# Fixed program order for TensorE from the third gMLP gate block to the last value block, with two S5 read-outs placed by hand

## Chip, core and metric

The kernel runs on one core of one Trainium2 chip. The metric is the device time of one execution in microseconds; "before" is the median of three runs, and one execution more was profiled.

## The reference

One decoder layer on 1024 tokens of width 1024, in fp32, as three sub-layers. Each is `x = x + rmsnorm(f(rmsnorm(x)))`. What matters here is the first one and the start of the second:

```python
h = rmsnorm(x, g_mix_pre)
s_in, s_gate, g_u, g_vv = split(h @ w_in)              # 4 x 512 columns
y_ssm  = gelu(s5_ssm(s_in, ...)) * sigmoid(s_gate)     # diagonal state space, 32 groups
y_gmlp = g_u * (tril(w_s) @ norm(g_vv) + b_s)          # per chunk of 128 positions
x = x + rmsnorm(concat(y_ssm, y_gmlp) @ w_out, g_mix_post)
mem_n = rmsnorm(mem, g_mem)                            # 256 memory tokens
k, v = mem_n @ w_k, mem_n @ w_v                        # for the cross-attention that follows
```

A gated ConvFFN ends the layer.

## The kernel before

**Layout.** Activations lie transposed, features on the partitions, tokens in two halves `h` of 512. Every fp32 matrix product is made of three fp32r products (hi x hi, hi x lo, lo x hi): `mm3` issues them, 24 for a block of eight 128-row parts. A weight tile comes by DMA into one of 4 `raw` slots; ScalarE casts it to its hi part (L132) and VectorE subtracts to get the lo part (L135), both into `w`, which has 13 slots. All DMAs are issued by SyncE (SP) from one queue, in order.

**S5.** The state space is computed in 8 batches of 4 groups by the generator `s5_batch`, in six steps: tables (VectorE and GpSimd), products and transposes into `px`, `pk`, the drive `pv`, rotation and scan (L588 to L600), turning back (L606 to L608), and the read-out: 8 products into an `sx` bank (L618, L619), which need L608. ScalarE then applies GELU (L621) and the result goes to memory as `yd`. `s5_all` starts a batch every second step, so the last read-outs, of batches 6 and 7, are traced in steps 17 and 19. For each block of 128 channels `s5_final` loads `yd` of two batches back in another layout (8 DMAs) with the sigmoid gate `gd`, multiplies (L659, half on VectorE, half on GpSimd), and splits the product into parts 0 to 3 of `mix`. Block 3 needs batches 6 and 7.

**The stage in question.** `mixers` runs in this order: columns for S5 and its gate, `gv`, gate blocks 0 and 1, mixing, gate blocks 2 and 3 (`gates(b)`, a product for each half, acc<-b), then 8 key blocks (acc<-m, 256 tokens wide) and 8 value blocks (acc<-w,m: 4 columns `c`, 2 memory halves `mt`). The memory is normalized in four pairs in `mem_parts` on VectorE (L686), ScalarE and GpSimd (L254, m<-sq,m), while the gates run. S5's steps, `mem_parts` and other side jobs advance by `tick`, called from `mm3`.

**Behind it.** `attention` begins with the output projection `o1`: 8 blocks for each half, which read the mix parts in the order 4, 5, 6, 7, 0, 1, 2, 3. Beside the first half GpSimd splits keys and values (`kv_parts`, kv<-m) and adds up tiles of the down-projection's weights for the last stage (`s_sums`: loads L1376, sums L1380, stores L1381). `sumsq` squares every block on ScalarE and adds the squares on GpSimd (L713, ac<-ac,sq); the total of the first half goes through TensorE (L281) while the second half's products run.

**What sets the order.** The kernel is traced, and a scheduler then orders every engine's queue by its own estimate of when operands are ready. An instruction given to `keep_in_program_order` is tied behind the one traced before it on its engine. `pin` does so, only while `self.pinned` is set, which is at the very end of the kernel. Engines run their queues in order.

Of the kernel before, what the change touches and what calls it, by code (L numbers as in the profile page):

```python
# [22 lines left out]
P = 128  # L23
# [17 lines left out]
WARM = 10  # L41
EARLY = 1
MIX_AT = 2
Q_STATS = (99, 3)
TAIL_R = (0, 7)
TAIL_B = (1, 3)
# [106 lines left out]
class Builder:  # L153
    def __init__(self, tc, a, out):
        self.tc = tc
        self.nc = tc.nc
        self.a = a
        self.out = out
        self.sides = []
        self.pools = []  # L160
        self.n_slot = 0
        self.pinned = False
        self.final_ok = False


    def slot(self, tag, dt=F32, shape=None):
# [56 lines left out]
    def pin(self, ins):  # L223

        if self.pinned:
            self.tc.keep_in_program_order(ins)

    def mm3(self, ps, parts, ticks=2, first=True, last=True, go_on=False):

        nc = self.nc  # L230
        n = len(parts)
        for i, (lh, ll, rh, rl) in enumerate(parts):
            for j, (x, y) in enumerate(((lh, rh), (lh, rl), (ll, rh))):
                self.pin(nc.tensor.matmul(ps, lhsT=x, rhs=y, start=first and i + j == 0,  # L234
                                          stop=last and i == n - 1 and j == 2, skip_group_check=go_on))
            if ticks and (i + 1) * ticks // n > i * ticks // n:
                self.tick()
# [297 lines left out]
    def s5_batch(self, b):  # L535

        nc, v, g = self.nc, self.nc.vector, self.nc.gpsimd
        g0 = 4 * b
        bq = 4 * (b % 2)
        gs = slice(g0, g0 + 4)  # L540
        q4 = lambda: self.slot("x", shape=[P, 4, P])

        def outer(o, A, B):
            t = q4()
            o4 = o.rearrange("p g (j c) -> p g j c", c=16)
            t4 = t.rearrange("p g (j c) -> p g j c", c=16)
            def av(x):
                return x[:, gs].unsqueeze(2).to_broadcast([P, 4, 8, 16])
            def bv(x):
                return x[:, :, gs].rearrange("p j g -> p g j").unsqueeze(3).to_broadcast([P, 4, 8, 16])  # L550
            v.tensor_tensor(o4, av(A[0]), bv(B[0]), ALU.mult)
            g.tensor_tensor(t4, av(A[1]), bv(B[1]), ALU.mult)
            v.tensor_tensor(o, o, t, ALU.add)
        xt = q4()
        outer(xt, self.s5_B, self.s5_G)
        yield
        px = self.bank("sx")
        pk = self.bank("sx")
        for i in range(4):
            nc.tensor.transpose(px[:, i * P:(i + 1) * P], xt[:, i], self.ident)  # L560
        for i in range(4):
            nc.tensor.matmul(pk[:, 16 * i:16 * i + 16], lhsT=xt[:, i], rhs=self.s5_c0[:, g0 + i], start=True, stop=True)
        x = q4()
        nc.scalar.copy(x.rearrange("p a b -> p (a b)"), px)
        ka = self.tiny([P, 16, 4], "s5ka", 2)
        v.tensor_tensor(ka, pk[:, :64].rearrange("p (g c) -> p c g", c=16),
                        self.s5_dd[:, gs].rearrange("p g c -> p c g"), ALU.add)
        kd = self.kd[b % 4]
        nc.sync.dma_start(kd[0:P], ka.rearrange("p c g -> p (c g)"))
        u = q4()  # L570
        nc.sync.dma_start(u, self.ud[b // 2].rearrange("j (c g) k -> (j c) g k", g=8)[:, bq:bq + 4])
        yield
        pv = self.bank("sx")
        for i in range(4):
            nc.tensor.matmul(pv[:, i * P:(i + 1) * P], lhsT=x[:, i], rhs=u[:, i], start=True, stop=True)
        vv = q4()
        nc.scalar.copy(vv.rearrange("p a b -> p (a b)"), pv)
        vs = q4()
        nc.sync.dma_start(vs[0:64], vv[64:P])
        nc.sync.dma_start(vs[64:P], vv[0:64])  # L580
        yield

        c, s, t = q4(), q4(), q4()
        f4 = lambda x: x.rearrange("p g (h l) -> p g h l", l=8)
        hv = lambda x: x[:, :, gs].rearrange("p h g -> p g h").unsqueeze(3).to_broadcast([P, 4, 16, 8])
        lv = lambda x: x[:, :, gs].rearrange("p l g -> p g l").unsqueeze(2).to_broadcast([P, 4, 16, 8])
        (lc, ls), (hc, hs) = self.s5_el, self.s5_eh
        g.tensor_tensor(f4(c), hv(hc), lv(lc), ALU.mult)  # L588
        g.tensor_tensor(f4(t), hv(hs), lv(ls), ALU.mult)
        v.tensor_tensor(c, c, t, ALU.subtract)  # L590
        t = q4()
        g.tensor_tensor(f4(s), hv(hc), lv(ls), ALU.mult)
        v.tensor_tensor(f4(t), hv(hs), lv(lc), ALU.mult)
        v.tensor_tensor(s, s, t, ALU.add)
        v.tensor_tensor(vv, vv, c, ALU.mult)
        v.tensor_tensor(vs, vs, s, ALU.mult)
        v.tensor_tensor(vv, vv, vs, ALU.add)
        w = t
        for i in range(4):
            v.tensor_tensor_scan(w[:, i], self.s5_r8[:, g0 + i:g0 + i + 1].to_broadcast([P, P]), vv[:, i], 0.0,  # L600
                                 ALU.mult, ALU.add)
        ws = vs
        nc.sync.dma_start(ws[0:64], w[64:P])
        nc.sync.dma_start(ws[64:P], w[0:64])
        yield
        v.tensor_tensor(w, w, c, ALU.mult)  # L606
        g.tensor_tensor(ws, ws, s, ALU.mult)
        v.tensor_tensor(w, w, ws, ALU.subtract)  # L608
        tz = self.slot("x", shape=[P, 8, 64])
        k0 = kd[0:1]  # L610
        nc.sync.dma_start(tz, bass.AP(k0.tensor, k0.offset, [[64, P], [16 * 64, 8], [1, 64]]))
        z = q4()
        outer(z, self.s5_C, self.s5_H)
        yield
        py = self.bank("sx")
        for i in range(4):
            o = py[:, i * P:(i + 1) * P]
            nc.tensor.matmul(o, lhsT=tz.rearrange("p j (c g) -> p (j c) g", g=4)[:, :, i], rhs=u[:, i], start=True, stop=False)  # L618
            nc.tensor.matmul(o[:, 1:P], lhsT=z[:, i], rhs=w[:, i, 0:P - 1], start=False, stop=True)  # L619
        y = q4()  # L620
        nc.scalar.activation(y.rearrange("p a b -> p (a b)"), py, AF.Gelu_apprx_tanh)  # L621
        nc.sync.dma_start(self.yd[b // 2].rearrange("j c g k -> (j c) g k")[:, bq:bq + 4], y)
        yield

    def s5_all(self):

        live = []
        b = 0
        step = 0
        while b < 8 or live:  # L630
            if b < 8 and step % 2 == 0:
                live.append(self.s5_batch(b))
                b += 1
            for gname in list(live):
                if next(gname, "end") == "end":
                    live.remove(gname)
            step += 1
            yield

    def s5_chain(self):  # L640
        yield from self.s5_all()
        while not self.final_ok:
            yield
        yield from self.s5_final()

    def s5_final(self):

        nc, v = self.nc, self.nc.vector
        for blk in range(4):
            y = [self.slot("k", shape=[P, 4, P]) for _ in range(2)]  # L650
            for j in range(8):
                nc.sync.dma_start(y[j // 4][:, j % 4], self.yd[blk][7 - j].rearrange("c g k -> (c g) k"))
            for h in range(2):
                sg = self.slot("k")
                nc.sync.dma_start(sg, self.gd[blk][h])
                sv = sg.rearrange("p (k j) -> p j k", j=8)
                for jh in range(2):
                    e = v if jh == 0 else nc.gpsimd
                    e.tensor_tensor(sv[:, 4 * jh:4 * jh + 4], y[jh][:, :, 64 * h:64 * h + 64],  # L659
                                    sv[:, 4 * jh:4 * jh + 4], ALU.mult)  # L660
                hl = self.mix[blk, h] = self.pair("b")
                self.split(*hl, sg)
                yield
# [233 lines left out]
    def mixers(self):  # L897
        nc, a, w, ids, xg = self.nc, self.a, self.w, self.ids, self.xg
        v, g = nc.vector, nc.gpsimd
# [4 lines left out]
        for kt in range(KT):  # L904
            if kt % 2 == 0:
                whi, wlo = w.get(ids["s01"][kt // 2])
            for h in range(2):
                hi, lo = hl = self.pair("b")
                x = self.xs[kt, h]
# [4 lines left out]
            for h in range(2):  # L914
                rh, rl = xg[h][kt]
                for b in range(2):
                    if kt == 0:
                        pss[b, h] = self.bank()
                    o = pss[b, h]
                    c = slice(256 * (kt % 2) + P * b, 256 * (kt % 2) + P * b + P)  # L920
# [38 lines left out]
        for b in range(4):  # L959
            part = self.blocks(ids["sg"][b])  # L960
            for h in range(2):
                ps = self.bank()
# [67 lines left out]
                mixing(b, h)  # L1030
        vt.clear()
        mem = self.side(self.mem_parts(), 1)
        for b in range(MIX_AT, 4):
            gates(b)
        xg[0], xg[1] = [], []
# [9 lines left out]
        for b in range(8):  # L1045
# [4 lines left out]
                self.kraw.append(self.slot("m", shape=[P, 2, 256]))  # L1050
            nc.scalar.copy(self.kraw[-1][:, b % 2], ps)
        for c in range(4):
            part = self.blocks(ids["v"][c], 256)
            for mt in range(2):
                ps = self.bank()[:, :256]
# [3 lines left out]
                nc.scalar.copy(self.vraw[mt, c // 2][:, 256 * (c % 2):256 * (c % 2) + 256], ps)  # L1059
        self.memp = None  # L1060
        self.drain(s5)


    def attention(self):
# [591 lines left out]
```

## Time and profile before

| | us |
|---|---|
| median of 3 runs (lowest, highest) | 1342.07 (1339.8, 1346.27) |
| profiled execution | 1340.39 |
| its span, first to last instruction | 1338.7 |
| TensorE busy in the span | 1270.3 |
| VectorE busy | 1062.5 |
| GpSimd busy | 691.0 |
| ScalarE busy | 628.3 |

Mean granted TensorE clock: 0.977. In a row of the trace stand start, length, engine, line, operation, out<-in, shapes, count, and in brackets the idle time ahead of it with what ended it. PE is TensorE, DVE VectorE, ACT ScalarE, POOL GpSimd. Lines are those of the kernel before; lines of the changed kernel stand 6 to 15 higher.

### The profile page before, as it was taken

How to read it: one execution, taken by the hardware profiler on the slowest of the kernel's cores; microseconds unless marked ns; L12 is line 12 of the kernel's file. 1: busy time of each engine (PE TensorE's matmuls, PEld its weight loads, DVE VectorE, ACT ScalarE, POOL GpSimd, SP SyncE). 2: the span in 40 equal slices, each digit the busy share in tenths (PEclk: the TensorE clock that was granted, in tenths of full speed). 3: DMA queues.
4: the chain of work that ended last, by engine and by line, in shares of the span. 5: the costliest groups of instructions: out<-in, count | busy, mean ns of one | idle time of the engine just before them, and what ended most of it. 6: DMA issues, size and time to landing. Idle time of an engine off the chain costs nothing. (4 is left out here: it accounts for less than half of the span.)

```text
span 1338.7 us, 19253 instructions
## 1 busy us (share of the span) xinstructions
PE 1270.3 (95%) x6356; PEld 1076.9 (80%) x6356; DVE 1062.5 (79%) x1627; ACT 628.3 (47%) x1176; POOL 691.0 (52%) x523
## 2 busy tenths in 40 slices
PE   9989998779999999889999999999999999999995
PEld 7778987678888788678888878888888888788885
DVE  7968989987558766996657988889998878995477
ACT  7233421245455444454545645555555555546341
POOL 1685445747644734630443838755565315763135
PEclk9989999879999999899999999999999999999997
DMA  9474435348826973451358566645555359666234
GB/s 319 139 206 113 114 95 166 86 125 306 288 94 200 319 244 89 125 187 56 91 163 296 162 222 233 186 144 161 154 167 164 103 162 379 190 201 210 72 92 157
DMA packets 150661, 233.56 MB, mean 174 GB/s; under 512 B 33697, under 2 KB 43041, under 8 KB 150561
## 3 DMA queue, kind: packets, MB, share of 16 engines
q1 hardware_dynamic: 150560, 232.34, 54.5%
q8 instruction: 49, 0.80, 0.3%
q14 instruction: 52, 0.42, 0.1%
HBM read 174.23 MB, written 53.85 MB: 170 GB/s over the span
## 5 line engine op out<-in xcount | busy, mean ns | idle before, releaser
L234 PE MATMUL acc<-b,w 128*128 128x512 f32 x2484 | 597.5, 393 | 10.0 <-DVE sq L965 3.4
L234 PEld LDWEIGHTS acc<-b,w 128*128 128x128 f32 x2484 | 466.6, 190 | 109.1 <-DVE sq L965 3.8
L135 DVE TENSOR_TENSOR w<-raw,w 128x512 fp32r<-128x512 f32 x206 | 203.9, 1000 | 92.6 <-PE acc L234 43.1
L234 PE MATMUL sx<-b,w 128*128 128x512 f32 x873 | 210.1, 390 | 0.7 <-ACT T L1303 0.6
L132 ACT CAST w<-raw 128x512 fp32r<-128x512 f32 x228 | 140.9, 621 | 132.7 <-PE acc L234 70.7
L234 PEld LDWEIGHTS sx<-b,w 128*128 128x128 f32 x873 | 163.6, 188 | 35.5 <-ACT T L1303 1.0
L234 PE MATMUL acc<-T,w 128*128 128x512 f32 x528 | 127.0, 389 | 0.0
L713 POOL TENSOR_TENSOR ac<-ac,sq 128x512 f32<-128x512 f32 x45 | 69.1, 1537 | 103.9 <-ACT sq L712 58.0
L234 PEld LDWEIGHTS acc<-T,w 128*128 128x128 f32 x528 | 99.1, 188 | 20.6
L254 DVE TENSOR_TENSOR w<-b,w 128x512 fp32r<-128x512 f32 x64 | 65.2, 1027 | 30.1 <-PE st L234 15.5
L731 POOL TENSOR_TENSOR m<-m,t 128x512 f32<-128x512 f32 x24 | 40.0, 1698 | 63.7 <-DVE m L730 50.7
L234 PE MATMUL sx<-T,w 128*128 128x512 f32 x264 | 66.5, 389 | 0.0
L234 PEld LDWEIGHTS sx<-T,w 128*128 128x128 f32 x264 | 49.6, 188 | 10.3
L712 ACT ACTIVATE sq<-m 128x512 f32<-128x512 f32 x66 | 41.0, 630 | 34.7 <-DVE ac L713 14.4
L116 POOL TENSOR_TENSOR st<-st,b 128x512 f32<-128x512 f32 x20 | 26.8, 1339 | 56.0 <-DMA st<-in_w_up 35.6
L1242 POOL TENSOR_TENSOR b<-b,m 128x512 f32<-128x512 f32 x22 | 32.2, 1466 | 44.9 <-ACT m L1241 44.7
L253 ACT CAST w<-b 128x512 fp32r<-128x512 f32 x64 | 39.6, 620 | 29.5 <-PE acc L234 18.1
L135 POOL TENSOR_TENSOR w<-raw,w 128x512 fp32r<-128x512 f32 x22 | 30.2, 1377 | 42.5 <-ACT w L132 24.7
L234 PE MATMUL acc<-w,b 128*128 128x256 f32 x384 | 49.3, 285 | 0.0
L1380 POOL TENSOR_TENSOR m<-m,m 128x512 f32<-128x512 f32 x28 | 39.3, 1410 | 18.9 <-DMA m<-in_w_dk 8.4
L730 DVE SCALAR_TENSOR_TENSOR m<-m,gains,st 128x512 f32<-128x512 f32 x32 | 44.5, 1457 | 3.3 <-ACT st L311 3.2
L234 PEld LDWEIGHTS acc<-w,b 128*128 128x128 f32 x384 | 47.0, 191 | 0.1
(360 smaller groups left out, 2335.5 us busy)
## 6 DMA issues: line engine op xcount, KB each, us to landing
raw<-in_w_up SPq DMA_DIRECT2D x68, 256.0 KB, 2.9
cd<-fd SPq DMA_DIRECT2D x44, 256.0 KB, 2.9
b<-sd SPq DMA_DIRECT2D x44, 256.0 KB, 3.9
b<-in_w_up SPq DMA_DIRECT2D x40, 256.0 KB, 2.8
raw<-in_w_out SPq DMA_DIRECT2D x32, 256.0 KB, 2.9
raw<-in_w_q SPq DMA_DIRECT2D x32, 256.0 KB, 2.8
raw<-in_w_o SPq DMA_DIRECT2D x32, 256.0 KB, 2.8
m<-in_w_dk SPq DMA_DIRECT2D x28, 256.0 KB, 4.7
```

The costliest lines, as they stand in the source:

```text
L116: g.tensor_tensor(p["S4"], p["12"], p["S2"], ALU.subtract)
L132: nc.scalar.copy(hi[:, :w], t[:, :w])
L135: e.tensor_tensor(lo[:, :w], t[:, :w], hi[:, :w], ALU.subtract)
L234: self.pin(nc.tensor.matmul(ps, lhsT=x, rhs=y, start=first and i + j == 0, stop=last and i == n - 1 and j == 2, skip_group_check=go_on))
L253: self.nc.scalar.copy(hi, src)
L254: (e or self.nc.vector).tensor_tensor(lo, src, hi, ALU.subtract)
L712: nc.scalar.activation(sq, src, AF.Square)
L713: (e or nc.gpsimd).tensor_tensor(acc, acc, sq, ALU.add)
L730: v.scalar_tensor_tensor(x, x, self.gain[gpost][:, i:i + 1], bc, ALU.mult, ALU.mult)
L731: g.tensor_tensor(x, x, rs, ALU.add)
L1242: nc.gpsimd.tensor_tensor(val, val, gate, ALU.mult)
L1380: g.tensor_tensor(t[to], t[x], t[y], op)
```

## The change

While `self.fixed` is set, from gate block 2 to the end of `mixers`, the products of `mm3` and of the read-outs keep the program's order. `s5_all` now halts at step 17 until the mix parts 4 to 7 are split (`final_ok`, just ahead of the key blocks), and at step 19 it first runs `s5_final` for blocks 0 to 2 and then halts until value column 2 begins (`v_ok`). Block 3 of `s5_final` follows at the end.

```diff
+V_AT = 2
...
+    def fix(self, ins):
+
+        if self.pinned or self.fixed:
+            self.tc.keep_in_program_order(ins)
...
-                self.pin(nc.tensor.matmul(ps, lhsT=x, rhs=y, start=first and i + j == 0,
+                self.fix(nc.tensor.matmul(ps, lhsT=x, rhs=y, start=first and i + j == 0,
...
         while b < 8 or live:
+
+            while step == 17 and not self.final_ok:
+                yield
+            if step == 19:
+                yield from self.s5_final(range(3))
+                while not self.v_ok:
+                    yield
...
     def s5_chain(self):
         yield from self.s5_all()
-        while not self.final_ok:
-            yield
-        yield from self.s5_final()
+        yield from self.s5_final(range(3, 4))
...
+        self.fixed = True
         for b in range(MIX_AT, 4):
             gates(b)
...
         for c in range(4):
+            self.v_ok = c >= V_AT
```

The order of instructions changes in one stretch of every queue and is the old one before and after it.

TensorE, read-out of batch 6 (sx), before: it stands in the last gate product, behind its first three instructions (b are the gates' operands).

```order
L234 MATMUL acc<-b_330,w_2512 128x512
L234 MATMUL acc<-b_331,w_2512 128x512
L234 MATMUL acc<-b_330,w_2513 128x512
L619 MATMUL sx<-x_1780,x_1827 128x127
L618 MATMUL sx<-x_1718,x_1825 128x128
L619 MATMUL sx<-x_1780,x_1827 128x127
L618 MATMUL sx<-x_1718,x_1825 128x128
L619 MATMUL sx<-x_1780,x_1827 128x127
L618 MATMUL sx<-x_1718,x_1825 128x128
L619 MATMUL sx<-x_1780,x_1827 128x127
L234 MATMUL acc<-b_358,w_2512 128x512
```

TensorE, the same read-out after the change (m are the normalized memory's pairs, m_2784 the last of them).

```order
L240 MATMUL acc<-m_2784,w_2560 128x256
L240 MATMUL acc<-m_2785,w_2560 128x256
L240 MATMUL acc<-m_2784,w_2561 128x256
L624 MATMUL sx<-x_1718,x_1825 128x128
L626 MATMUL sx<-x_1780,x_1827 128x127
L624 MATMUL sx<-x_1718,x_1825 128x128
L626 MATMUL sx<-x_1780,x_1827 128x127
L624 MATMUL sx<-x_1718,x_1825 128x128
L626 MATMUL sx<-x_1780,x_1827 128x127
L624 MATMUL sx<-x_1718,x_1825 128x128
L626 MATMUL sx<-x_1780,x_1827 128x127
L240 MATMUL acc<-m_2714,w_2704 128x256
```

It now follows the whole of key block 0. All 72 gate products from the second half of gate block 2 on, and key block 0, run ahead of it.

TensorE, read-out of batch 7, before: in the middle of key block 5.

```order
L234 MATMUL acc<-m_2793,w_3177 128x256
L234 MATMUL acc<-m_2794,w_3177 128x256
L619 MATMUL sx<-x_1860,x_1901 128x127
L618 MATMUL sx<-x_1808,x_1899 128x128
L619 MATMUL sx<-x_1860,x_1901 128x127
L618 MATMUL sx<-x_1808,x_1899 128x128
L619 MATMUL sx<-x_1860,x_1901 128x127
L618 MATMUL sx<-x_1808,x_1899 128x128
L619 MATMUL sx<-x_1860,x_1901 128x127
L234 MATMUL acc<-m_2793,w_3178 128x256
```

After: among the value products (w is the first operand there), between the two memory halves of value column 2.

```order
L240 MATMUL acc<-w_3454,m_2784 128x256
L240 MATMUL acc<-w_3455,m_2784 128x256
L240 MATMUL acc<-w_3454,m_2785 128x256
L624 MATMUL sx<-x_1808,x_2989 128x128
L626 MATMUL sx<-x_2940,x_2991 128x127
L624 MATMUL sx<-x_1808,x_2989 128x128
L626 MATMUL sx<-x_2940,x_2991 128x127
L624 MATMUL sx<-x_1808,x_2989 128x128
L626 MATMUL sx<-x_2940,x_2991 128x127
L624 MATMUL sx<-x_1808,x_2989 128x128
L626 MATMUL sx<-x_2940,x_2991 128x127
L240 MATMUL acc<-w_3409,m_2714 128x256
```

It moves from ahead of 61 key products and all values to behind all keys and five of the eight value blocks; three value blocks are left behind it. On VectorE and GpSimd batch 7's rotation and scan move behind the splits of more key weights and of mix parts 4 to 7, and blocks 0 to 2 of `s5_final` come earlier.

GpSimd, the output projection's first half, before (t<-t are the sums of down-projection weights, ac<-ac,sq the sums of squares of blocks 1 to 7).

```order
L1380 TENSOR_TENSOR t_3919<-t_3919,t_3917 128x512
L1380 TENSOR_TENSOR t_4023<-t_4021,t_4023 128x512
L713 TENSOR_TENSOR ac_3691<-ac_3691,sq_3748 128x512
L1380 TENSOR_TENSOR t_4021<-t_4017,t_4021 128x512
L1380 TENSOR_TENSOR t_4017<-t_4023,t_4017 128x512
L1380 TENSOR_TENSOR t_4019<-t_4019,t_4017 128x512
L713 TENSOR_TENSOR ac_3691<-ac_3691,sq_3806 128x512
L713 TENSOR_TENSOR ac_3691<-ac_3691,sq_3864 128x512
L713 TENSOR_TENSOR ac_3691<-ac_3691,sq_3914 128x512
L713 TENSOR_TENSOR ac_3691<-ac_3691,sq_3964 128x512
L713 TENSOR_TENSOR ac_3691<-ac_3691,sq_4014 128x512
L713 TENSOR_TENSOR ac_3691<-ac_3691,sq_4064 128x512
```

After:

```order
L1395 TENSOR_TENSOR t_3809<-t_3815,t_3809 128x512
L1395 TENSOR_TENSOR t_3917<-t_3923,t_3917 128x512
L725 TENSOR_TENSOR ac_3691<-ac_3691,sq_3914 128x512
L1395 TENSOR_TENSOR t_3811<-t_3811,t_3809 128x512
L1395 TENSOR_TENSOR t_4023<-t_4021,t_4023 128x512
L1395 TENSOR_TENSOR t_3919<-t_3919,t_3917 128x512
L725 TENSOR_TENSOR ac_3691<-ac_3691,sq_3964 128x512
L1395 TENSOR_TENSOR t_4021<-t_4017,t_4021 128x512
L725 TENSOR_TENSOR ac_3691<-ac_3691,sq_4014 128x512
L1395 TENSOR_TENSOR t_4017<-t_4023,t_4017 128x512
L1395 TENSOR_TENSOR t_4019<-t_4019,t_4017 128x512
L725 TENSOR_TENSOR ac_3691<-ac_3691,sq_4064 128x512
```

All sums of squares but one stood behind the weight sums; now the two are mixed to the end, and the last square's sum, which L281 reads, follows all 16 weight sums. In SP's queue the loads of those weights move behind ten of the projection's first weight tiles.

More of the change, by code (lines that the diff above doesn't have):

```diff
@@ L162, in __init__ @@
         self.pinned = False
-        self.final_ok = False
+        self.final_ok = self.v_ok = self.fixed = False
     def slot(self, tag, dt=F32, shape=None):
@@ L617, in s5_batch @@
             o = py[:, i * P:(i + 1) * P]
-            nc.tensor.matmul(o, lhsT=tz.rearrange("p j (c g) -> p (j c) g", g=4)[:, :, i], rhs=u[:, i], start=True, stop=False)
-            nc.tensor.matmul(o[:, 1:P], lhsT=z[:, i], rhs=w[:, i, 0:P - 1], start=False, stop=True)
+            self.fix(nc.tensor.matmul(o, lhsT=tz.rearrange("p j (c g) -> p (j c) g", g=4)[:, :, i], rhs=u[:, i],
+                                      start=True, stop=False))
+            self.fix(nc.tensor.matmul(o[:, 1:P], lhsT=z[:, i], rhs=w[:, i, 0:P - 1], start=False, stop=True))
         y = q4()
@@ L641, in s5_chain, with s5_final @@
         yield from self.s5_all()
-        while not self.final_ok:
-            yield
-        yield from self.s5_final()
-    def s5_final(self):
+        yield from self.s5_final(range(3, 4))
+    def s5_final(self, blocks):
         nc, v = self.nc, self.nc.vector
-        for blk in range(4):
+        for blk in blocks:
             y = [self.slot("k", shape=[P, 4, P]) for _ in range(2)]
@@ L1061, in mixers @@
         self.drain(s5)
+        self.fixed = False
     def attention(self):
```

## Prediction

> **What bounds the kernel now.** I read the page's busy shares first, then the table of stretches, the list of who waited for whom on TensorE, and last TensorE, VectorE and GpSimd in order of time where the change begins.
>
> ```profile
> PE 1270.3 (95%) x6356; PEld 1076.9 (80%) x6356; DVE 1062.5 (79%) x1627; ACT 628.3 (47%) x1176; POOL 691.0 (52%) x523
> 227.00:328.00 101.00, 81.73 (x519) 76.00 (x518) 86.55 (x87) 38.30 (x75) 66.39 (x44) 0.88 0.53 165
> 233.00:255.00 22.00, 12.11 (x53) 9.77 (x54) 21.34 (x26) 4.32 (x8) 15.05 (x11) 0.87 0.40 106
> 264.00:291.00 27.00, 19.13 (x131) 18.23 (x130) 26.33 (x26) 12.19 (x25) 18.36 (x11) 0.86 0.32 97
> PE sx L619 <- DVE x L608: 17.1, 5, 9.9
> PE acc L234 <- DVE w L135: 7.2, 7, 2.6
> ```
>
> TensorE bounds the kernel as a whole, but not from 227 to 328 us, where the change lies: there it idles 19 us in 101 (81.73 busy). In the rows of stretches the length is followed by the busy times of TensorE, its weight loads, VectorE, ScalarE and GpSimd, then the granted clock and the DMA columns. VectorE has 21.34 of 22.00 us and 26.33 of 27.00 us: in this stage it is the full engine, and TensorE waits for it. Of the read-outs' waits (17.1 us in all) 13.7 are the last two.
>
> ```profile
> 232.98 11.82 PE L234 MATMUL acc<-b,w 128*128 128x512 f32 x51
> 254.69 0.80 PE L619 MATMUL sx<-x,x 128*128 128x127 f32 x2 [9.89 <-DVE x L608]
> 257.76 5.85 PE L234 MATMUL acc<-b,w 128*128 128x512 f32 x21
> 265.13 7.79 PE L234 MATMUL acc<-m,w 128*128 128x256 f32 x63
> 290.79 0.80 PE L619 MATMUL sx<-x,x 128*128 128x127 f32 x2 [3.83 <-DVE x L608]
> 293.86 8.97 PE L234 MATMUL acc<-m,w 128*128 128x256 f32 x61
> 302.66 13.84 PE L234 MATMUL acc<-w,m 128*128 128x256 f32 x114
> 327.98 0.63 PE L234 MATMUL acc<-b,w 128*128 128x512 f32 x2
> 330.02 50.88 PE L234 MATMUL acc<-b,w 128*128 128x512 f32 x223 [1.42 <-DVE w L135]
> 380.75 0.95 PE L281 MATMUL st<-ones,ac 128*128 128x1 f32 x8
> ```
>
> acc<-b is a gate (to 263 us) or the output projection (from 328 us), acc<-m a key block, acc<-w,m a value block, sx a read-out. One product costs 11.82/51 = 0.232 us in the gates, 50.88/223 = 0.228 in the projection, 13.84/114 = 0.121 in the values. L281 is the sum of squares of the projection's first half: the last place that the change can move against its neighbours, since the order of every engine is the old one from about there.
>
> **Read-out 6 goes behind key block 0.** The 9.89 us wait for it disappears. What is late next is key block 0 itself.
>
> ```profile
> 259.78 1.29 POOL L254 TENSOR_TENSOR m<-sq,m 128x512 fp32r<-128x512 f32 x1
> 254.56 2.89 DVE L686 SCALAR_TENSOR_TENSOR sq<-sq,gains,ac 128x256 f32<-128x256 f32 x2
> ```
>
> 72 gate products are left at 232.98, so the gates end at 232.98 + 72 x 0.232 = 249.7. Key block 0 needs all of the normalized memory, and its last quarter is written by GpSimd until 261.07, from what VectorE ends at 257.45. Nothing on VectorE, GpSimd or ScalarE ahead of these rows is moved, and VectorE is full there. In program order TensorE therefore stands in key block 0, in three pieces, for 261.07 + 5 x 0.124 - 249.7 - 24 x 0.124 = 9.0 us (0.124 = 7.79/63) and ends it at 261.7. The read-out behind it (257.76 - 254.69 = 3.07 us) ends at 264.8. Before, key block 1 began at 265.13 + 13 x 0.124 = 266.7. Gain here: 1.9 us of the 9.9.
>
> **The key blocks** are fed by VectorE, whose queue is now: more weights first, batch 7's rotation and scan later.
>
> ```profile
> 260.45 1.62 DVE L593 TENSOR_TENSOR x<-k,k 128x512 f32<-128x512 f32 x1
> 281.09 2.45 DVE L600 TENSOR_TENSOR_SCAN x<-r,x 128x128 f32<-128x128 f32 x4
> 286.56 0.69 DVE L606 TENSOR_TENSOR x<-x,x 128x512 f32<-128x512 f32 x1 [0.64 <-DMA x<-x]
> 294.27 0.68 DVE L135 TENSOR_TENSOR w<-raw,w 128x512 fp32r<-128x512 f32 x1
> ```
>
> From 260.45 to 294.9 VectorE worked without a pause but the 0.64. By the time it splits the last weight of value block 0 it has, in the new order, done the same instructions less L606 and L608 (1.3 us) and that pause, plus three more splits (1.8): 294.8. A weight load starts when the split four places back is done, and by that two of these splits come up to 0.9 late: 295.7. This is a reordering of a full engine; the weights' waits in the key blocks grow by what the read-outs' waits shrink. Value block 0's last six products follow: 296.4, against 302.66 + 24 x 0.121 = 305.6 before. The gain is 9.2 us at this point.
>
> **Value blocks and read-out 7.** VectorE is ahead from here. Read-out 7 at full clock took 2.5 us:
>
> ```profile
> 221.73 0.49 PE L619 MATMUL sx<-x,x 128*128 128x127 f32 x2
> 224.21 2.07 PE L1013 MATMUL acc<-k,m 128*64 128x128 f32 x26
> ```
>
> Products after a wait are slow for a time: 61 took 8.97 us where 0.121 each gives 7.4, so I put 1.5 us on the first blocks. Four blocks (24 x 0.121 = 2.9 each), 1.5 and 2.5 put the read-out's end at 312.0; three more blocks end the values at 320.8. From there 225 products x 0.228 lead to L281: 372.1, against 380.75. Were TensorE alone, the gain would be 8.6 us.
>
> **What hangs on read-out 7.** It ended at 293.86 and will end at 312.0, 18 us later. Its chain is y to memory, eight loads back, gate, split into the last parts of the mix, and then on GpSimd the splits of keys and values and the sums of the down-projection's weights.
>
> ```profile
> 310.29 0.68 DVE L254 TENSOR_TENSOR b<-k,b 128x512 fp32r<-128x512 f32 x1
> 312.03 7.64 POOL L254 TENSOR_TENSOR kv<-m,kv 128x512 fp32r<-128x512 f32 x5 [3.36 <-ACT kv L253]
> 329.38 4.68 POOL L1380 TENSOR_TENSOR t<-t,t 128x512 f32<-128x512 f32 x3
> 334.01 3.00 POOL L254 TENSOR_TENSOR kv<-m,kv 128x512 fp32r<-128x512 f32 x2
> 336.99 7.86 POOL L1380 TENSOR_TENSOR t<-t,t 128x512 f32<-128x512 f32 x5
> 344.80 1.74 POOL L713 TENSOR_TENSOR ac<-ac,sq 128x512 f32<-128x512 f32 x1
> 346.51 4.68 POOL L1380 TENSOR_TENSOR t<-t,t 128x512 f32<-128x512 f32 x3
> 351.15 1.28 POOL L713 TENSOR_TENSOR ac<-ac,sq 128x512 f32<-128x512 f32 x1
> 375.25 1.29 POOL L713 TENSOR_TENSOR ac<-ac,sq 128x512 f32<-128x512 f32 x1 [4.15 <-ACT sq L712]
> t<-in_w_dk SPq DMA_DIRECT2D x16, 256.0 KB, 5.4
> POOL m L1380 <- DMA m<-in_w_dk: 8.4, 2, 4.6
> L1380 POOL TENSOR_TENSOR m<-m,m x28: 1265/1295/1808, 432.4 to 484.5; 128x512 f32<-128x512 f32 x28
> ```
>
> The last mix part is ready 310.29 + 0.68 - 293.86 = 17.1 us after the read-out (about 16.6 for the first half of the tokens, which goes first). TensorE asks for it 72 x 0.121 + 35 x 0.228 = 16.7 us after: 0, at most 1 us.
>
> GpSimd is the term that decides. Its run of 8 key/value splits, 16 weight sums and 7 sums of squares (31 in a row, the last one needed by L281) began 312.03 - 293.86 = 18.2 us after the read-out; before, it was through by 352.43 but for sums that waited on TensorE, the last at 376.5, 4.2 us ahead of L281. Now it begins at 312.0 + 18.2 = 330.2, with the sums of squares among the rest. Beside the projection's weight splits, 15 of these instructions took 352.43 - 329.38 = 23.05 us, 1.54 each; 31 take 47.6 us: 377.8. TensorE stands at L281 from 372.1, 5.7 us. Bounds: 1.29 (375.25's row, alone) gives 370.2 and no wait; 1.74 (344.80's) gives 384.1. I take 1.54, the same work in the same stage. L281 then runs 380.75 - 377.8 = 3.0 us earlier than before.
>
> After a wait of 9.89 us the 21 products took 5.85 us instead of 21 x 0.228 = 4.8 and the read-out 3.07 instead of 2.5: 1.6 us. The new wait costs the same; bounds 0 and 2.1 (read-out 7 and the 61 products, after 3.83 us).
>
> Sum: -8.6 + 5.7 + 1.6 = -1.3 us, and from there the old order shifts as a whole. The profiled execution takes 1340.39 us (span 1338.7 and 1.7 around it), inside the runs' 1339.8 to 1346.27; it would take 1339.1. Against the median of 1342.07: 1340.8. About 0.5% (6.7 us) is what a measurement of this kernel can tell from no change.
>
> **Rivals.**
> *GpSimd keeps up* (faster). At 1.35 us each or less its 31 end by 372.1, and the whole 8.6 stays: 1333.5. For it: the later weight sums (the last row above, ns: least, median, most) have a median of 1.295 us. Against: 15 in 23.05 us here.
>
> *VectorE and GpSimd exclude each other* (no change, on the slow side). Each projection block brings two weight splits on VectorE, about 0.60 each when they follow each other, per 5.5 us. If none overlapped with GpSimd, 31 x 1.29 + 17 x 0.60 = 50.2 us, L281 at 380.4 and with the slow products +1.3: 1343.4. In 329.38 to 352.43 that sum gives 15 x 1.29 + 9 x 0.6 = 24.8, measured 23.05: most of it, not all. This is what the Trainium skill says in "SBUF — State Buffer", section "Who interferes with whom": a VectorE instruction with two SBUF inputs and a GpSimd one that reads SBUF share an exclusive lock. By that rule the time is the 1343.4 above; the trace shows slightly less.
>
> *GpSimd starves* (slower). The 16 weight-sum loads now stand in SP's queue behind the projection's weights, the last ones behind stores that wait for GpSimd. Each lands 5.4 us after its issue. If three of the four groups of loads hold GpSimd for 3.5 us, L281 comes 10.5 us later: 1351. It decides slower from 8 us of such waits. For it: GpSimd waited 8.4 us for two such loads later in the old kernel (the row of L1380 above). Against: each group of loads stands in the queue among the stores of the groups before it, so it is asked for while GpSimd still works on those.
>
> **How the numbers follow.** My forecast 0.53 (1340.8; own range 1336 to 1345), exclusion 0.15 (1343.4), GpSimd keeps up 0.21 (1333.5), starving 0.11 (1351). Faster by over 0.5%: the third and its like, 0.21; slower: the last, 0.11; within: 0.68. Range 1333 to 1347, which leaves out most of the starving case and half of the fast one's tail.
>
> **What would show it.** The profile after should have no wait of sx on L608 over 1 us from 233 us on; waits inside key block 0 for GpSimd and ScalarE, together near 9 us; L281 waiting some 6 us on GpSimd's L713; the values' end near 321 us, L281 near 378. I am wrong if L281 does not wait (the gain stays), if GpSimd has pauses for loads of w_dk, or if the key blocks' weights come before 290 us.

## The result, and the profile after

The changed kernel takes 1335.96 us (median of 17 runs, 1333.73 to 1341.39), the kernel before in the same session 1344.87 (17 runs, 1338.65 to 1352.68): ratio 0.9939, 95% interval 0.9922 to 0.9955, which is 8.2 us less (6.1 to 10.5). The forecast was 1340.8.

TensorE in order of time, after the change (start, length, count; in brackets the wait and what ended it). Lines have moved: L240 is the product, L287 the sum of squares (L281 before), L314 the next small product (L308 before).

```profile
249.06 1.59 PE L240 MATMUL acc<-m,w 128*128 128x256 f32 x12
...
254.19 1.44 PE L240 MATMUL acc<-m,w 128*128 128x256 f32 x5 [2.93 <-POOL m L260]
258.21 0.58 PE L240 MATMUL acc<-m,w 128*128 128x256 f32 x1 [2.58 <-ACT m L259]
261.14 1.43 PE L240 MATMUL acc<-m,w 128*128 128x256 f32 x5 [2.34 <-POOL m L260]
...
265.72 11.05 PE L240 MATMUL acc<-m,w 128*128 128x256 f32 x86
278.13 1.70 PE L240 MATMUL acc<-m,w 128*128 128x256 f32 x12 [1.37 <-DVE w L136]
281.52 3.13 PE L240 MATMUL acc<-m,w 128*128 128x256 f32 x24 [1.69 <-DVE w L136]
...
291.71 15.18 PE L240 MATMUL acc<-w,m 128*128 128x256 f32 x120
...
309.38 8.87 PE L240 MATMUL acc<-w,m 128*128 128x256 f32 x72
318.09 51.19 PE L240 MATMUL acc<-b,w 128*128 128x512 f32 x225
372.15 1.44 PE L287 MATMUL st<-ones,ac 128*128 128x1 f32 x8 [2.87 <-POOL ac L725]
373.46 10.58 PE L240 MATMUL acc<-b,w 128*128 128x512 f32 x33
383.87 1.05 PE L314 MATMUL st<-ident,rs_y 128*128 128x128 f32 x8
```

The 9.89 us wait for read-out 6 is gone. In its place key block 0 stands for 2.93, 2.58 and 2.34 us and, in a row left out, 0.23: 8.1 us. The key blocks then run with 4.3 us of waits for weights; the two longest are shown. The value blocks begin at 291.71, the projection at 318.09 (327.98 before). Behind its first half stands a new wait of 2.87 us for GpSimd's sum, and then 33 products that take 10.58 us where 33 x 0.228 gives 7.5.

The rows of stretches (TensorE, its weight loads, VectorE, ScalarE, GpSimd, then the granted clock):

```profile
227.00:328.00 101.00, 88.57 (x562) 80.96 (x562) 83.62 (x95) 41.75 (x83) 53.43 (x35) 0.93 0.53 157
264.00:291.00 27.00, 22.75 (x173) 21.94 (x173) 25.98 (x26) 13.62 (x29) 16.91 (x10) 0.95 0.42 122
```

From 227 to 328 TensorE is busy 88.57 us instead of 81.73. VectorE still has 25.98 of the 27 us from 264 to 291: the stage is still VectorE's, but TensorE gets 173 products into it instead of 131.

GpSimd behind read-out 7 (multiplication of the read-back, then key and value splits, the weight sums L1395, the sums of squares L725):

```profile
319.25 1.32 POOL L671 TENSOR_TENSOR k<-k,k 128x256 f32<-128x256 f32 x1 [21.51 <-DMA k<-gd]
321.42 1.38 POOL L671 TENSOR_TENSOR k<-k,k 128x256 f32<-128x256 f32 x1 [0.85 <-DMA k<-gd]
325.50 7.66 POOL L260 TENSOR_TENSOR kv<-m,kv 128x512 fp32r<-128x512 f32 x5 [2.70 <-ACT kv L259]
333.12 1.74 POOL L1395 TENSOR_TENSOR t<-t,t 128x512 f32<-128x512 f32 x1
...
370.38 1.72 POOL L725 TENSOR_TENSOR ac<-ac,sq 128x512 f32<-128x512 f32 x1
```

31 operations from 325.50 to 372.10, without a pause: 1.50 us each. The last one, at 370.38, is what L287 waits for.

| us | before | before, second profile | after | same order, second profile |
|---|---|---|---|---|
| projection begins | 327.98 | 329.20 | 318.09 | 318.63 |
| sum of squares, L281/L287 (wait) | 380.75 (0) | 381.54 (0) | 372.15 (2.87) | 371.90 (2.09) |
| L308/L314 | 389.18 | 389.97 | 383.87 | 380.44 |
| projection ends (its second L281/L287) | 435.51 | 436.33 | 430.13 | 426.71 |
| profiled execution | 1340.39 | 1344.77 | 1341.39 | 1337.95 |

The two profiles first compared do not show a gain in their totals (1340.39 and 1341.39), though at the projection's end the changed kernel is 5.4 us ahead. The second profiles, from the first two experiments below, tell why.

### The profile page after: what moved, and what is told of

The parts are those of the page before. It is cut to its first block, busy times and chain, and to the rows that moved or that the text cites. A ratio compares the mean times of both kernels' runs of the same rounds, so it can differ in the third digit from the quotient of the medians.

```text
span 1339.4 us, 19263 instructions
## 1 busy us (share of the span) xinstructions
PE 1272.3 (95%) x6356; PEld 1078.0 (80%) x6356; DVE 1058.7 (79%) x1627; ACT 628.3 (47%) x1176; POOL 690.1 (52%) x523
## 5 line engine op out<-in xcount | busy, mean ns | idle before, releaser
L240 PE MATMUL acc<-b,w 128*128 128x512 f32 x2484 | 597.6, 394 | 7.5 <-ACT t L1318 2.4
L240 PEld LDWEIGHTS acc<-b,w 128*128 128x128 f32 x2484 | 467.7, 190 | 106.6 <-DVE b L749 3.3
L136 DVE TENSOR_TENSOR w<-raw,w 128x512 fp32r<-128x512 f32 x206 | 197.9, 969 | 98.0 <-PE acc L240 46.2
L240 PE MATMUL sx<-b,w 128*128 128x512 f32 x873 | 212.5, 393 | 2.1 <-ACT T L1318 2.1
L240 PEld LDWEIGHTS sx<-b,w 128*128 128x128 f32 x873 | 165.4, 190 | 37.6 <-ACT T L1318 2.5
L240 PE MATMUL acc<-T,w 128*128 128x512 f32 x528 | 127.0, 389 | 0.0
L240 PEld LDWEIGHTS acc<-T,w 128*128 128x128 f32 x528 | 99.1, 188 | 20.6
L725 POOL TENSOR_TENSOR ac<-ac,sq 128x512 f32<-128x512 f32 x45 | 69.4, 1545 | 85.6 <-issue 45.1
L240 PE MATMUL sx<-T,w 128*128 128x512 f32 x264 | 66.5, 389 | 0.0
L240 PEld LDWEIGHTS sx<-T,w 128*128 128x128 f32 x264 | 49.6, 188 | 10.3
L259 ACT CAST w<-b 128x512 fp32r<-128x512 f32 x64 | 39.5, 619 | 29.0 <-PE acc L240 18.2
L1395 POOL TENSOR_TENSOR m<-m,m 128x512 f32<-128x512 f32 x28 | 39.2, 1404 | 21.5 <-DMA m<-in_w_dk 20.0
L240 PE MATMUL acc<-w,b 128*128 128x256 f32 x384 | 49.3, 285 | 0.0
L240 PEld LDWEIGHTS acc<-w,b 128*128 128x128 f32 x384 | 47.0, 191 | 0.1
```

Of the source, the lines that this page charges most:

```text
L136: e.tensor_tensor(lo[:, :w], t[:, :w], hi[:, :w], ALU.subtract)
L240: self.fix(nc.tensor.matmul(ps, lhsT=x, rhs=y, start=first and i + j == 0, stop=last and i == n - 1 and j == 2, skip_group_check=go_on))
L259: self.nc.scalar.copy(hi, src)
L725: (e or nc.gpsimd).tensor_tensor(acc, acc, sq, ALU.add)
L1395: g.tensor_tensor(t[to], t[x], t[y], op)
```

## The experiments

Ratios are to the kernel before, measured beside it on the same chip; in brackets the 95% interval. The experiments ran on three chips, so ratios are compared here, not times.

**The tie against the placement.** The change ties products to the program's order and places two read-outs. Here the tie is left out.

```diff
-        self.fixed = True
+        self.fixed = False
```

> The two halts of the S5 generator and the split of its last read-backs are kept; the products are no longer tied to the program's order. Theory: the placement does it all and the tie does nothing, since the instruction order that comes out is the same as the changed kernel's on all five engines: ratio to the kernel before 0.994 (0.991 to 0.997), the sum of squares (L287) near 372 us with a wait of 2 to 4 us for GpSimd, L314 near 384. Rival: the tie matters, for what it keeps from moving: ratio 1.000, L287 near 380. It is at the same time a second profile of the changed order: if the wait for ScalarE's copy near 717 us (2.1 us, then 2.4 us of slow products) comes again, the loss there belongs to the change; if it is 0.6 us as before the change, it belongs to that one execution.

Measured: 1337.27 us, ratio 0.9939 (0.9919 to 0.9959), the same as with the tie.

```profile
371.90 1.05 PE L287 MATMUL st<-ones,ac 128*128 128x1 f32 x8 [2.09 <-POOL ac L725]
372.82 7.79 PE L240 MATMUL acc<-b,w 128*128 128x512 f32 x33
380.44 1.05 PE L314 MATMUL st<-ident,rs_y 128*128 128x128 f32 x8
```

The placement is the whole change; the tie moves nothing. (The tie alone, without the halts, was not run.) L287 waits 2.09 us here and the 33 products behind it take 7.79: the 3 us of slow products in the first profile are not in every execution. The wait near 717 us came again (1.95 us).

**The kernel before, once more.** No edit.

> The kernel before, unchanged, for a second profile and for what a measurement of no change gives. The two profiles so far, of before and after the change, differ by -8.6 us at L281/L287, by -5.3 at L308/L314 and by +1.1 near 1300 us, where the medians of 17 runs each differ by -8.9. Theory: the change does nothing behind 450 us; the first profile of before is a fast execution (1340.4 against a median near 1345), and the later losses belong to single executions: this profile has the same landmarks within 1 us up to 450 (L281 380 to 381.5, L308 388.5 to 390) and loses 2 to 6 us between 690 and 1300. Rival: the change brings losses behind 450 us of its own: this profile again passes 1300 us near 1299, and the medians' 8.9 is then not explained by the window. Ratio 1.000 (0.997 to 1.003) in both.

Measured: ratio 1.0003 (0.9986 to 1.0021). TensorE's wait for ScalarE's copy, in the first profile of before and in the second:

```profile
721.24 0.50 PE L234 MATMUL sx<-b,w 128*128 128x512 f32 x1 [0.62 <-ACT T L1303]
```
```profile
720.76 0.50 PE L234 MATMUL sx<-b,w 128*128 128x512 f32 x1 [1.74 <-ACT T L1303]
```

From the projection's begin to its end the two agree within 1.2 us. At 720 the second has the longer wait, and it passes the last stage's sum of squares 3.3 us later than the first (1302.38 against 1299.04). So the first profile of before was a short execution in its later part, and what the first profile of after "lost" at 717 is a loss that both kernels can have. The gain is in the window: 9.9 and 10.6 us at the projection's begin, 5.4 to 9.6 at its end.

**Without the halt at step 17.** Read-out 6 comes where the generator's pace puts it.

```diff
-            while step == 17 and not self.final_ok:
-                yield
```

> The changed kernel without the halt at step 17: read-out 6 comes some 180 products earlier, among the products ahead of the gates, and VectorE does the chain of batch 6 earlier and the memory later; the place of read-out 7 stays. Theory: VectorE is full until 295 and the order of its work in there is nearly neutral, so what counts is the place of read-out 7 alone: the values end within 2 us of 318, L287 within 3 us of 372, ratio 0.994 to 0.997. Rival: the place of read-out 6 carries a part of its own, as the prediction had it with 1.9 us or more: the wait goes to the earlier read-out or to the gates, the values end 4 us or more later, ratio 0.998 or more.

Measured: 1347.37 us, ratio 1.0005 (0.9987 to 1.0023).

```profile
217.12 1.11 PE L566 MATMUL sx<-ident,x 128*128 128x128 f32 x4 [5.06 <-DVE x L559]
...
239.80 0.80 PE L626 MATMUL sx<-x,x 128*128 128x127 f32 x2 [12.29 <-DVE x L614]
...
256.18 3.68 PE L1023 MATMUL acc<-k,m 128*64 128x128 f32 x32 [4.36 <-DVE sq L1028]
```

The rival holds. TensorE stands 5.06 us at a transpose, 12.29 at read-out 6 (239.80) and 4.36 in the mixing, and behind that goes through gates, keys and values without a wait. The projection begins near 331.6, 13.5 us later than after the change. At the projection's end this profile is 6.7 to 7.5 us behind the two of before, and it stays behind: it passes the last stage's sum of squares at 1307.81 (1299.04 and 1302.38) and takes 1348.49 us (1340.39 and 1344.77). The medians lie closer, 1347.37 and 1345.72 on that chip; where the other executions win the rest back no trace shows.

**Without the halt at step 19.** Read-out 7 comes right behind key block 1, and the read-backs of blocks 0 to 2 move to the end with block 3.

```diff
-            if step == 19:
-                yield from self.s5_final(range(3))
-                while not self.v_ok:
-                    yield
...
-        yield from self.s5_final(range(3, 4))
+        yield from self.s5_final(range(4))
```

> The changed kernel without the halt at step 19 and with the four read-backs of S5 together at the end: read-out 6 stays behind key block 0, read-out 7 comes right behind key block 1, with the products in fixed order. VectorE then does batch 7's rotation and scan ahead of ten of the weight splits; the read-out's input is ready near 288 and TensorE, which is there at 268.7, waits 17 to 20 us; the six key blocks and the value blocks behind it run at TensorE's own pace (18 + 2 + 24 us): values end 330 to 336. Theory: without a late place for read-out 7 the wait is back and larger: L287 at 383 to 388, ratio 1.002 to 1.006. Rival: the gain is that of read-out 6 (its halt alone): ratio 0.995 or less, values' end 320 or less.

Measured: 1362.74 us, ratio 1.0138 (1.0102 to 1.0174).

```profile
294.05 0.80 PE L626 MATMUL sx<-x,x 128*128 128x127 f32 x2 [21.76 <-DVE x L614]
...
345.48 5.63 PE L240 MATMUL acc<-b,w 128*128 128x512 f32 x24
```

The theory held in kind and was over 10 us short in size. The read-out's input was ready at 294, not 288, and the value and projection blocks behind it waited 6 us for ScalarE's and VectorE's halves of weights that had been put off. Each halt is needed: with only one of them the change gains nothing or loses some 18 us.

**Read-out 7 earlier.** In front of the fourth of eight value products' blocks, not the sixth.

```diff
-V_AT = 2
+V_AT = 1
```

> The changed kernel with read-out 7 in front of the fourth of the eight value products' blocks instead of the sixth (V_AT 1). The read-out ends 48 products, 6.1 us, earlier, near 303.5; its input was ready at 298.9, so it does not wait. Theory: the mix, the splits and GpSimd's run of about 31 operations follow the read-out: GpSimd starts at 319 to 320 instead of 325.5, the last sum of squares is ready before 369 and L287 does not wait: L314 near 378, ratio to the kernel before 0.990. Rival: GpSimd's start is set by ScalarE's copies of the keys and values, which come at the values' end, not by the read-out: start stays within 1 us of 325.5, the wait stays near 2.9, ratio 0.994.

Measured: 1331.29 us, ratio 0.9897 (0.9877 to 0.9917). GpSimd:

```profile
320.89 8.11 POOL L260 TENSOR_TENSOR kv<-m,kv 128x512 fp32r<-128x512 f32 x5 [2.93 <-ACT kv L259]
...
369.82 1.28 POOL L725 TENSOR_TENSOR ac<-ac,sq 128x512 f32<-128x512 f32 x1 [3.19 <-ACT sq L724]
```

GpSimd's splits start at 320.89, 4.6 us earlier for a read-out that ends 5.5 us earlier (the values go on behind it at 303.88, not 309.38), and the last sum stands at 369.82 waiting for ScalarE's square, not for its place in the queue. L287 waits 0.58 us. This beats both kernels.

**Read-out 7 later**, by as much.

```diff
-V_AT = 2
+V_AT = 3
```

> The changed kernel with read-out 7 in front of the last value product's block (V_AT 3), 48 products and 6.1 us later than in the changed kernel. Theory: mix and GpSimd follow the read-out one for one: the last mix part comes near 330.5 and TensorE, which asks for it near 325, waits 4 to 6 us in the projection's first block; GpSimd's run starts near 331.5, its last sum is ready near 378; L287 at 376 to 379, L314 at 385 to 390; ratio to the kernel before 0.997 to 1.000. Rival: the 16 us between read-out and mix have slack (the read-back is no longer beside value weights): wait below 2 us, L314 below 384, ratio 0.994.

Measured: 1339.58 us, ratio 0.9974 (0.9955 to 0.9993). GpSimd's splits, and TensorE at L287:

```profile
331.24 8.20 POOL L260 TENSOR_TENSOR kv<-m,kv 128x512 fp32r<-128x512 f32 x5 [1.32 <-ACT kv L259]
```
```profile
377.96 1.86 PE L287 MATMUL st<-ones,ac 128*128 128x1 f32 x8 [4.15 <-POOL ac L725]
```

GpSimd starts at 331.24 (331.5 forecast) and L287 is at 377.96 (376 to 379). The forecast wait of 4 to 6 us for the last mix part did not come. TensorE's order had changed: 241 products instead of 225 stand ahead of L287, and none of them waits. So the late read-out is paid for once, at L287, and 16 products less are left behind it: at the projection's end (431.57) this run is 1.4 us behind the first profile after the change.

**Fewer GpSimd operations ahead of the sum.** The weight sums' generator is advanced in the projection's second half.

```diff
-                if h == 0:
+                if h == 1:
                     next(s_job)
```

> The changed kernel, with the weight sums of the down-projection advanced during the second half of the output projection and no longer during the first. TensorE, VectorE and ScalarE keep their order exactly; on GpSimd four weight sums move from ahead of the last sum of squares to behind it. Theory: GpSimd's run sets the wait at L287. Four sums of 1.5 us each less: the last sum of squares is ready at 366.1 instead of 372.1, TensorE gets to L287 at 369.3 and does not wait, and the 3.0 us of slow products behind it go too: L314 near 378 instead of 383.9; ratio to the kernel before 0.990. Rival: the wait is set by something else (the squares of ScalarE, the loads of the sums) and stays at 2 to 3 us: ratio 0.994. Second rival: the wait goes but the next stage takes it back, where TensorE waits for VectorE near 449 us: L314 near 378, ratio 0.994.

Measured: 1334.99 us, ratio 0.9920 (0.9904 to 0.9937). GpSimd:

```profile
356.67 1.28 POOL L725 TENSOR_TENSOR ac<-ac,sq 128x512 f32<-128x512 f32 x1
361.83 4.36 POOL L1395 TENSOR_TENSOR t<-t,t 128x512 f32<-128x512 f32 x3 [3.88 <-DMA t<-in_w_dk]
...
369.09 1.71 POOL L725 TENSOR_TENSOR ac<-ac,sq 128x512 f32<-128x512 f32 x1
```

The wait at L287 fell to 0.92 us (2.87 and 2.09 in the two profiles of the changed order) and not to 0: the loads of the weight tiles are now asked for later, and GpSimd paused 3.88 us for one. The four operations saved were worth 6 us and the pause took 3.9 of them. The 33 products behind the wait took 9.38 us. The pause is the prediction's starving rival, which the change itself did not have. The time is not apart from the changed kernel's.

**The same wait, cut elsewhere.** The first half's seven sums of squares go to VectorE.

```diff
-            self.sumsq(t, sq[h], b == 0)
+            self.sumsq(t, sq[h], b == 0, v if name == "o1" and h == 0 else None)
```

> The changed kernel with the seven sums of squares of the projection's first half on VectorE instead of GpSimd. Theory: GpSimd's run was the wait at L287, and nothing else holds the sum: TensorE does not wait there (below 0.3 us), no slow products behind it, L314 near 378 (380.4 and 383.9 in the two profiles of the changed order); GpSimd is done with its splits and weight sums 10 us earlier; ratio to the kernel before 0.991 (0.989 to 0.993). Rival: VectorE, which shares the time with GpSimd, becomes late with weight splits in the projection: new waits of TensorE on L136 between 318 and 372 that eat the gain, ratio 0.994 or more.

Measured: 1333.38 us, ratio 0.9918 (0.9889 to 0.9946).

```profile
369.62 1.05 PE L287 MATMUL st<-ones,ac 128*128 128x1 f32 x8 [0.79 <-DVE ac L725]
...
378.14 1.05 PE L314 MATMUL st<-ident,rs_y 128*128 128x128 f32 x8
```

L287 now waits 0.79 us for VectorE, L314 comes at 378.14 as forecast, and no new waits for weights appeared ahead of it. GpSimd's run was the wait; what is left of it was forecast below 0.3. The interval of the ratio overlaps the changed kernel's, so the gain is read from the trace.

**Both.** V_AT 1 and the sums on VectorE.

> Both of the edits that made the changed kernel faster: read-out 7 in front of the fourth block of values (V_AT 1) and the seven sums of squares on VectorE. Theory: they remove the same wait at L287, so they do not add up: that wait was down to 0.6 and 0.8 us with either, L314 near 377.5 to 379.7, ratio to the kernel before 0.988 to 0.991. Rival: they add, ratio 0.986 or less (0.9897 and 0.9918 each alone, against 0.9939).

Measured: 1331.73 us, ratio 0.9912 (0.9890 to 0.9934); L287 at 369.36 without a wait, L314 at 377.77. They remove one and the same wait and do not add.

**Splits on the full engine.** With V_AT 1 VectorE is full until 291. The next three runs ask what GpSimd's work costs it there. In the run with V_AT 1, stretches with GpSimd busy and idle, and VectorE's rows in each:

```profile
263.00:281.00 18.00, 15.22 (x113) 14.81 (x111) 17.21 (x12) 10.93 (x23) 17.38 (x10) 0.91 0.39 115
281.00:291.00 10.00, 8.33 (x65) 7.92 (x66) 9.48 (x17) 3.52 (x8) 0.00 (x0) 1.00 0.51 140
```
```profile
276.11 1.95 DVE L136 TENSOR_TENSOR w<-raw,w 128x512 fp32r<-128x512 f32 x1
...
281.96 0.68 DVE L136 TENSOR_TENSOR w<-raw,w 128x512 fp32r<-128x512 f32 x1
```

The same subtraction takes 1.95 us beside GpSimd and 0.68 (0.60 from start to start) alone.

```diff
-                self.split(*hl, gu.pop((b, h)), g)
+                self.split(*hl, gu.pop((b, h)))
```

> The changed kernel with V_AT 1 and the eight splits of the mix parts 4 to 7 (b<-m,b) on VectorE instead of GpSimd, in the stretch around 250 to 275 us where VectorE is the full engine. TensorE's order stays. Theory: VectorE and GpSimd hold each other up there (12 VectorE operations took 17.2 us beside 10 GpSimd operations of 17.4 us from 263 to 281; with GpSimd idle the same kind takes 0.60 each): a split costs 1.3 us on GpSimd and 0.6 on VectorE out of the same time, so the move frees about 8 x 0.66 = 5 us: waits of TensorE for key weights fall from 5.4 to below 2.5 us, values end 314 to 316.5 instead of 318.3, ratio 0.985 to 0.988. Rival: the engines work beside each other and VectorE, which is full, gets 8 x 0.6 = 4.8 us more: weights later, values end 321 to 323, ratio 0.992 to 0.994.

Measured: 1330.69 us, ratio 0.9898 (0.9878 to 0.9919).

```profile
277.50 13.61 PE L240 MATMUL acc<-m,w 128*128 128x256 f32 x94 [4.50 <-DVE w L136]
...
316.71 0.63 PE L240 MATMUL acc<-b,w 128*128 128x512 f32 x2
```

Eight operations more on the full engine, and the projection begins 1.6 us earlier (318.34 with them on GpSimd), not 2.7 to 4.7 later: the rival fell. The theory's 2 to 4 us came only in part: one wait of 4.50 us for a key weight is left, behind the products that prepare batch 7's rotation, on which both engines still work together. The time did not move.

With the memory's splits moved as well:

```diff
-            self.split(*hl, m, g)
+            self.split(*hl, m)
```

> As the run with the eight mix splits on VectorE, and the four splits of the normalized memory (m<-sq,m) there too. Theory: beside the 5 us of the mix splits, 4 x 0.66 = 2.6 us more, and key block 0 is no longer held by GpSimd's last memory split at 261.1: the waits in key block 0 fall from 6.2 us to 3 to 4, it ends near 258 to 260 instead of 262.4; values end 312 to 315; ratio 0.983 to 0.987. Rival: VectorE's extra 2.4 us come ahead of the same memory parts and key block 0 ends where it did or later: no gain over the run with the mix splits alone.

Measured: 1326.60 us, ratio 0.9872 (0.9853 to 0.9891), the lowest here, though its interval overlaps those of V_AT 1 alone and of the mix splits alone.

```profile
314.36 0.63 PE L240 MATMUL acc<-b,w 128*128 128x512 f32 x2
...
366.21 1.05 PE L287 MATMUL st<-ones,ac 128*128 128x1 f32 x8
```

The projection begins 4.0 us earlier than with V_AT 1 alone, and L287 does not wait. TensorE gets there at 366.2; with V_AT 1 alone at 371.16 - 0.58 = 370.6.

With the memory's splits alone:

> V_AT 1 with only the four memory splits (m<-sq,m) on VectorE; the mix splits stay on GpSimd. It is the fourth corner of the square: neither 0.9897, mix splits alone 0.9898, both 0.9872. Theory: the memory splits are what pays, because key block 0 waits for them and not for the mix splits: it ends near 259 (262.4 with neither, 259.9 with the mix splits alone, 258.1 with both), ratio to the kernel before 0.986 to 0.988. Rival: only both together pay, since with the mix splits on GpSimd the key weights stay late (VectorE's 1.7 to 1.9 us each until 281): key block 0 ends earlier, but the values' end stays at 317 to 318.5, ratio 0.989 to 0.991.

Measured: 1333.49 us, ratio 0.9917 (0.9888 to 0.9947).

```profile
316.95 0.73 PE L240 MATMUL acc<-b,w 128*128 128x512 f32 x2
```

Neither forecast fits whole. TensorE gets to L287 at 369.1, 1.5 us earlier than with V_AT 1 alone; with the mix splits alone it is 1.2 (370.13 - 0.70 = 369.4), with both 4.4. By the traces each move helps and both together give more than the sum; why more is open, and the times of the single moves do not tell them from V_AT 1 alone.

## Why the prediction was right or wrong

The time lies in the range (1333 to 1347) and just below the forecast's own (1336 to 1345). That it came so near is partly luck: the kernel before, measured beside it, took 1344.87 us and not the 1342.07 from which the forecast started, and from 1342.07 the ratio 0.9939 leads to 1333.9. The likeliest case was "no measurable change" (-1.3 us), and -0.61% (-8.2 us) is a gain by the bound that was set. Which engine waits for which was foreseen; three terms were mis-sized. Step by step, from the first profile after:

- **Read-out 6 behind key block 0**: right in what waits and for how long; the block waited 8.1 us (9.0). The block and the read-out ran longer than forecast, so the read-out ended at 266.1 (264.8) and key block 1 began 1.0 us earlier than before (1.9).
- **Key blocks**: undersized. The first value block ended at 291.71 + 24 x 0.1265 = 294.7, not 296.4: a gain of 10.9 us, not 9.2. VectorE had this block's last weight ready near 294.0, not at 295.7. It paused for 1.1 us, near the 0.9 put on for late loads, but its instructions took about 2 us less than forecast. The scans of batch 7 show half of that, 1.36 us where the row of before has 2.45, at a place where GpSimd is now idle:

```profile
291.42 1.36 DVE L606 TENSOR_TENSOR_SCAN x<-r,x 128x128 f32<-128x128 f32 x4
```

  So reordering a full engine was not neutral, as the prediction took it to be: how long an instruction lasts depends on what GpSimd does beside it (the subtraction of 1.95 and 0.68 us above). The last key weight was ready near 289.2, ahead of the 290 that was named as a sign of being wrong.
- **Value blocks**: undersized. The 1.5 us for a slow clock were 0.7 (120 products in 15.18 us against 14.5). Read-out 7 ended at 309.6 (312.0), values at 318.1 (320.8), and TensorE stood at L287 at 372.15 - 2.87 = 369.3 (372.1). The gain of TensorE alone was 11.5 us, not 8.6. The key and value blocks together are the first term that was mis-sized.
- **The last mix part**: right, no wait.
- **GpSimd's run**: its length was right (1.50 us each against 1.54), its start wrong: 325.50, not 330.2. 2.4 us come from the earlier read-out; 2.3 from the chain behind it, which took 15.9 us and not the 18.2 copied from before. It shrank in its first step, the store of read-out 7's result. SyncE issued it 1.5 us behind the read-out before (at 295.35) and 0.7 after (at 310.29), and it landed sooner (before and after; size, then us from issue to landing):

```profile
yd<-x SPq DMA_DIRECT2D x1, 256.0 KB, 3.7
```
```profile
yd<-x SPq DMA_DIRECT2D x1, 256.0 KB, 2.2
```

  The loads behind it thus began 2.9 us behind the read-out (at 312.53) instead of 5.2 (at 299.11), which is the whole 2.3. The multiplications began 12.5 us behind the read-out before (306.40 - 293.86, the row below) and 9.6 after (319.25 - 309.6); from there to GpSimd's splits the chain took 0.6 us more.

```profile
306.40 2.27 POOL L659 TENSOR_TENSOR k<-k,k 128x256 f32<-128x256 f32 x2 [18.03 <-DMA k<-gd]
```

  That is the second mis-sized term: a chain through memory was moved and its old length kept. With both, L287 waited 2.87 and 2.09 us, not 5.7.
- **Slow products behind that wait**: 3.05 us in one profile, 0.3 in the other, against 1.6. This third term is not one number.

The sum: -11.5 + 2.9 + 3.05 = -5.6 at L314 in the first profile (-5.3 measured). The second profile of the changed order is 8.7 us ahead of the first of before at L314, and the runs show -8.2. The forecast had -1.3.

Rivals: "GpSimd keeps up" came nearest in time, and not by its mechanism, since the operations took 1.50 us and not 1.35; the run began earlier and the wait was half the size. "Exclude each other" gave 50.2 us for the run, which took 46.6. "Starves" did not happen in the changed kernel. Of the signs named, no read-out wait and 8 us in key block 0 came true; the L287 wait near 6, the values' end at 321 and L281 at 378 did not. One thing was not asked at all: whether the tie to the program's order does anything. Beside the halts it does not.

## What to carry to other kernels

When a step moves, re-derive the length of the chain behind it too: its transfers can be asked for and land sooner or later at the new place, and a copied 18.2 us hid 2.3 us of gain here. Move the releaser and count the queue that it releases: the same read-out placed 6 us earlier took another 0.4% off, placed 6 us later gave back about half the gain, because 31 operations of another engine started with it. And take a second profile of both kernels before reading a difference of 1 us in totals: here the window of both pairs showed the gain (5.4 and 9.6 us at its end, 8.2 in the runs), and the totals of the first pair did not.

## What was not expected of the hardware

VectorE and GpSimd together took almost the sum of their times alone: with V_AT 1, from 263 to 281 us, 12 VectorE operations took 17.21 and 10 of GpSimd 17.38 us out of 18; one by one (0.60 and 1.29 us each) they would need 20. Moving 12 splits from GpSimd to the engine that was already full brought TensorE to L287 4.4 us earlier in its profile. The Trainium skill, "SBUF — State Buffer", section "Who interferes with whom", calls it an exclusive lock between a VectorE instruction with two SBUF inputs and GpSimd's reads; these runs agree but for a tenth of overlap.

The clock was granted at half after a short wait, and not after another of nearly its length. From 374 to 378 us, behind the wait of 2.87 us in the changed kernel and behind 2.09 in the same order's second profile (the last three columns are the granted clock, the DMA share and GB/s):

```profile
374.00:378.00 4.00, 4.00 (x11) 3.10 (x10) 2.06 (x10) 0.62 (x1) 0.00 (x0) 0.50 0.36 128
```
```profile
374.00:378.00 4.00, 4.00 (x20) 3.27 (x19) 2.22 (x10) 1.87 (x4) 0.00 (x0) 1.00 0.42 132
```

The Trainium skill, "TensorE: Matmul & The Clock Gate", section "HAM oscillation — how this bites in real kernels", warns of idle gaps above about 3.4 us. Here one of 2.87 us was enough, and it cost 3 us more than itself. Nor does the length of the wait alone decide: with the late weight sums the same 33 products took 9.38 us behind a wait of 0.92. What decides is open.
